# Triangular solves on GpSimd, spare buffers for two heads, and the S5 setup's copies on ScalarE, in a decoder trunk

## The chip, the core and the metric

The kernel runs on one core of a Trainium2 chip. The core has a matrix engine (TensorE, PE), a vector engine (VectorE, DVE), a scalar engine (ScalarE, ACT), GpSimd (POOL) and SyncE (SP), which issues most of the transfers. The metric is the time of one execution in microseconds on the device. Before the change three runs took 1185.95 to 1189.26 us, median 1188.44.

## The reference

One layer of a hybrid decoder trunk on 1024 tokens of width 1024, in float32. A normalised input is projected once into the inputs of three branches: an RG-LRU, a gated DeltaNet (GDN) with 8 heads of 128, and a diagonal complex state space (S5). Their outputs go through gates, are joined, projected back, added to the input, and a small gated embedding follows. What matters here is the GDN head:

```python
kb = kc * bc[..., None]
a_kk = jnp.where(strict, jnp.einsum('nbhid,nbhjd->nbhij', kb, kc) * decay, 0.0)
lhs = a_kk + jnp.eye(c, dtype=jnp.float32)
sol = lax.linalg.triangular_solve(lhs, rhs, left_side=True, lower=True, unit_diagonal=True)
u_c, w_c = sol[..., :dv], sol[..., dv:]
...
def step(state, inp):
    v_new = u_i - jnp.einsum('bhcd,bhde->bhce', w_i, state)
    o_i = (q_i * exp(gc_i)) @ state + aqk_i @ v_new
    state = state * jnp.exp(g_last)[..., None, None] + jnp.einsum('bhcd,bhce->bhde', k_dec, v_new)
    return state, o_i
_, o = lax.scan(step, state0, (qc, kc, u_c, w_c, a_qk, gcum))
```

The scan is a chain: a step needs the state of the step before. The triangular systems and the products with q and k don't depend on the state.

## The kernel before

The kernel holds its data with the channel in the partition. A projection block (`project`) is 48 matmuls of 128x512 in fp32r: 8 slices of the width, three products each (high half by high half, low by high, high by low), for two halves of the tokens; its operands are called hhi, hlo, whi, wlo and its result pp. The blocks of the RG-LRU and S5 inputs come first, with the S5 branch computed between them, then the blocks k 0, 1, 2, q 0, v 0 and z 0, and then, head by head in `gdn`, k of head h+3, q, v and z of head h+1.

Between the matmuls of a projection a planner, written into the kernel itself, puts all other work. It prices each instruction (`price`), keeps a modelled time for each engine (`account`), and at each projection matmul (`fill`, `tick`) advances the tasks whose modelled inputs are there, by priority (`PRIO`). `need(tasks)` lets the projections stop until the tasks named are done. A task yields a letter for the lane on which it goes on ("v" DVE, "a" ACT, "g" GpSimd, "pe" PE, "d" transfers). The order that comes out is fixed on every engine, so each engine takes its instructions strictly in that order. Every change in a price, an engine or a wait moves the order of everything behind it.

For a GDN head the tasks are these.
- `project_conv` evacuates a block into raw, after a fill of three columns on GpSimd (L486), and runs a convolution of four taps on DVE (L477); the SiLU on ACT gives kT or qT.
- `k_post` makes AT on DVE (L1131) and writes the 32x32 diagonal blocks of two heads to memory.
- `solve(h0)`, for two heads at a time, inverts the diagonal blocks in 31 rounds of a multiplication (L1156) and a subtraction (L1159) on 64 partitions. Round j works on n x m elements with n = j+1, m = 31-j; over all rounds that is 5,456 elements twice. It runs on DVE before (SOLVE_G = 8, that is for no head on GpSimd). GpSimd prepares W with a fill and a mask (L1147, L1148).
- `levels(h)` builds the inverse of the whole 128x128 blocks from them on PE (matmuls M,XT and Xs,AT; Xs is written by DVE, L1234).
- `chain(h)` is the recurrence, two chunks of 64 at a time, so eight steps t: Sm·kT on PE, R on DVE (L1293), XT·R on PE, V on DVE (L1305), V·kd on PE, and the new Sm on DVE (L1317). The parts of the output, Sm·qT and V·AQ, stand beside them on PE. I call each passage from DVE back to PE a hop: three per step.

`gdn` calls `need(*prev)`, with prev the chain of head h, ahead of k_proj(h+3) and q_proj(h+1): the four buffers of kT and two of qT are reused, and at h = 1 they belong to head 0. So k_proj(4) and q_proj(2) start when chain(0) is done.

The S5 setup (`s5_base`) computes small tables on DVE; its 17 copies and sign changes are `cpy` (L803) and `ng` (L802). The gates are in `gates`: two products with gg on PE, then egl, ekd, egc on ACT (L585 to L589); they use the single PSUM buffer pc, as the transposes of s_Q (L902 copies them out) do. Before the convolution of S5 the input u goes to memory and back in another layout (ud, s_U), and the kernel row Kp becomes the Toeplitz matrices s_MT. `decay` makes the masks of the GDN decay: it loads gcb and masks it on GpSimd (L609).

## Time and profile before

The profiled execution took 1193.25 us; its span is 1191.5 us, the rest lies around the span. The granted clock of TensorE is 0.968 in the mean.

| | before |
|---|---|
| median of 3 runs | 1188.44 us |
| profiled execution | 1193.25 us |
| its span | 1191.5 us |
| PE busy | 1112.1 us (93%) |
| DVE busy | 784.9 us (66%) |
| ACT busy | 565.7 us (47%) |
| GpSimd busy | 158.8 us (13%) |
| mean granted clock | 0.968 |

PE is busy nearly all the time. Its 79 us of idle time stand in a few places, 9.1 of them at the very start. The clock of PE is at its full level (2.4 GHz) for most of the span and at the half (1.2 GHz) in some stretches after idle time. When PE has little to do its clock falls, and the first matmuls of what follows run at the low clock; in the rows below such a tail is seen from the duration of a 128x512 matmul, 0.63 us instead of 0.40.

In a row of the timeline the first number is the start in us from the start of the span, the second is the duration, then engine, line, operation, output and inputs, shape, and how many like it follow each other. In brackets stands the idle time of the engine before it, and what ended it.

### The profile page before, as it was taken

To read this page: it belongs to the slowest core of one execution; us is meant where nothing else is said; L and a number is where in the kernel's file an instruction comes from. 1 tells how busy PE (TensorE), PEld (TensorE's weight loads), DVE (VectorE), ACT (ScalarE), POOL (GpSimd) and SP (SyncE) were. 2 spreads that over 40 slices of the span, in tenths; PEclk is the share of its full clock that TensorE was granted. 3 is DMA by queue.
4 is the path that set the end of the run, shared out by engine and by line. 5 is a ranking of instruction groups with operands and counts; after the bars stand their busy time and mean duration, and the time that the engine had idled before them with its cause. 6 is when DMAs were issued, how large, how long until landed. Compare 5 with 4: busy or idle time off the path is not lost. (4 is left out here: it accounts for less than half of the span.)

```text
span 1191.5 us, 17246 instructions
## 1 busy us (share of the span) xinstructions
PE 1112.1 (93%) x6165; PEld 903.9 (76%) x6165; DVE 784.9 (66%) x1933; ACT 565.7 (47%) x1138; POOL 158.8 (13%) x166
## 2 busy tenths in 40 slices
PE   6889688999989899999999999999989899999996
PEld 4677476777878677788888888878867688878885
DVE  6787576857578786786678667865655444263665
ACT  6533536634767784244543545344663143253332
POOL 1100000000011010000000010000053042044441
PEclk9999889999989999699999999999999999999999
DMA  8311354555567331122222221212355564464222
GB/s 301 119 36 45 99 134 140 144 152 132 157 192 210 115 125 33 48 71 54 94 67 72 54 94 32 89 33 74 117 161 211 194 212 159 142 210 134 71 90 88
DMA packets 85222, 140.18 MB, mean 118 GB/s; under 512 B 31760, under 2 KB 42192, under 8 KB 85136
## 3 DMA queue, kind: packets, MB, share of 16 engines
q1 hardware_dynamic: 83984, 134.88, 36.7%
q0 software_dynamic: 1152, 4.19, 0.9%
q8 instruction: 49, 0.80, 0.3%
q14 instruction: 37, 0.30, 0.1%
HBM read 97.98 MB, written 31.49 MB: 109 GB/s over the span
## 5 line engine op out<-in xcount | busy, mean ns | idle before, releaser
L195 PE MATMUL pp<-hhi,whi 128*128 128x512 f32 x768 | 316.3, 412 | 4.4 <-ACT hhi L404 2.3
L195 PE MATMUL pp<-hlo,whi 128*128 128x512 f32 x768 | 314.3, 409 | 3.1 <-DVE hlo L407 3.1
L195 PE MATMUL pp<-hhi,wlo 128*128 128x512 f32 x768 | 315.1, 410 | 1.8 <-DVE wlo L425 1.8
L195 PEld LDWEIGHTS pp<-hhi,whi 128*128 128x128 f32 x768 | 147.4, 192 | 35.9 <-ACT hhi L404 3.3
L195 PEld LDWEIGHTS pp<-hlo,whi 128*128 128x128 f32 x768 | 147.1, 192 | 33.4 <-DVE hlo L407 4.0
L195 PEld LDWEIGHTS pp<-hhi,wlo 128*128 128x128 f32 x768 | 147.1, 191 | 30.9 <-issue 2.4
L477 DVE SCALAR_TENSOR_TENSOR cy<-raw,c_gdn_conv_w,cy 128x512 f32<-128x512 f32 x144 | 108.2, 752 | 15.0 <-ACT cy L473 12.2
L1508 DVE TENSOR_TENSOR mhl<-mr,mhl 128x512 fp32r<-128x512 f32 x64 | 61.5, 963 | 76.4 <-ACT mhl L1506 76.3
L195 PE MATMUL pg<-ws,mhl 128*128 128x512 f32 x384 | 102.6, 401 | 0.2 <-DVE mhl L1508 0.2
L425 DVE TENSOR_TENSOR wlo<-wraw,whi 128x1024 fp32r<-128x1024 f32 (+1 forms) x52 | 62.5, 1201 | 47.0 <-ACT whi L423 45.4
L1508 POOL TENSOR_TENSOR ws<-wsr,ws 128x512 fp32r<-128x512 f32 x48 | 67.2, 1403 | 181.7 <-ACT ws L1506 181.5
L195 PEld LDWEIGHTS pg<-ws,mhl 128*128 128x128 f32 x384 | 72.3, 190 | 18.0 <-DVE mhl L1508 1.0
L195 PE MATMUL pp<-ws,fth 128*128 128x512 f32 x256 | 81.3, 397 | 0.0
L1506 ACT CAST mhl<-mr 128x512 fp32r<-128x512 f32 x64 | 39.8, 621 | 77.3 <-DMA mr<-mix 45.6
L487 ACT COPY raw<-pp 128x512 f32<-128x512 f32 x56 | 32.7, 584 | 82.6 <-PE pp L195 82.5
L423 ACT CAST whi<-wraw 128x1024 fp32r<-128x1024 f32 (+1 forms) x52 | 52.7, 1014 | 26.5 <-DMA wraw<-in_w_blk 26.0
L195 PE MATMUL pp<-ws,mhl 128*128 128x512 f32 x192 | 53.3, 405 | 5.3 <-ACT mhl L1506 2.6
L195 PEld LDWEIGHTS pp<-ws,fth 128*128 128x128 f32 x256 | 48.0, 188 | 10.9
L1506 ACT CAST ws<-wsr 128x512 fp32r<-128x512 f32 x48 | 29.8, 623 | 54.2 <-DMA wsr<-in_w_out 22.9
L1331 ACT ACTIVATE osq<-on 128x128 f32<-128x128 f32 x64 | 19.8, 309 | 70.5 <-DVE on L1328 53.7
L195 PE MATMUL pp<-ws,ftl 128*128 128x512 f32 x128 | 51.1, 400 | 0.0
L195 PEld LDWEIGHTS pp<-ws,mhl 128*128 128x128 f32 x192 | 35.5, 190 | 15.5 <-ACT mhl L1506 3.0
(414 smaller groups left out, 2018.1 us busy)
## 6 DMA issues: line engine op xcount, KB each, us to landing
wraw<-in_w_blk SPq DMA_DIRECT2D x48, 512.0 KB, 4.2
mr<-mix SPq DMA_DIRECT2D x64, 256.0 KB, 3.0
dec<-dec SPq DMA_DIRECT2D x16, 512.0 KB, 4.5
wsr<-in_w_out SPq DMA_DIRECT2D x32, 256.0 KB, 2.9
xt<-in_xT SPq DMA_DIRECT2D x16, 256.0 KB, 5.9
ppd<-po POOLq DMA_DIRECT2D x8, 512.0 KB, 3.4
gcb<-grow SPq DMA_DIRECT2D x8, 512.0 KB, 4.8
dec<-gcb SPq DMA_DIRECT2D x8, 512.0 KB, 2.8
```

The costliest lines, as they stand in the source:

```text
L195: self.nc.tensor.matmul(**kw)
L423: nc.scalar.copy(out=hi, in_=raw)
L425: nc.vector.tensor_tensor(out=lo, in0=raw, in1=hi.bitcast(F32), op=ALU.subtract)
L477: nc.vector.scalar_tensor_tensor(out=y[:, sl], in0=raw[:, j + sl.start:j + sl.stop], scalar=wconv[:, j:j + 1], in1=y[:, sl], op0=ALU.mult, ...
L487: nc.scalar.copy(out=raw[:, 3 + 512 * half:3 + 512 * half + 512], in_=ps)
L1331: nc.scalar.activation(out=sq, in_=on[:, t, :], func=AF.Square, accum_out=d["so"][:, t:t + 1])
L1506: nc.scalar.copy(out=hl[:, 0, :], in_=raw)
L1508: e.tensor_tensor(out=hl[:, 1, :], in0=raw, in1=hl[:, 0, :].bitcast(F32), op=ALU.subtract)
```

## The change

There are three parts.

1. `SOLVE_G` is 0 instead of 8: all four `solve` tasks emit their 62 operations to GpSimd instead of DVE.
2. `extra` gives three buffers of the size of kT from a pool of their own ("more"). Head 4 takes its kT and head 2 its qT from it, and the gates of the S5 output projection (`glu`) take the three that were in a pool "gsig". At h = 1 `need(*prev)` is asked for only ahead of v_proj(2), not ahead of k_proj(4) and q_proj(2). For the other heads the order of calls stays. `q_post(h)` now also waits for chain(h-2), the last reader of q's second-level buffer.
3. In `s5_base` the four fills of 1.0 and 0.0 go to GpSimd, and the 17 copies and sign changes to ScalarE, with `yield` of the lane so that the planner counts them there.

```diff
--- before.py
+++ after.py
@@ -29,7 +29,7 @@
 HEADS = 8
 GATE = 0
 SHARED = (3, 7)
-SOLVE_G = 8
+SOLVE_G = 0
 SQRT_2PI = 0.7978845608028654
 
 
@@ -272,6 +272,9 @@
     def slot(self, tag, shape, name, dtype=F32):
         return self.wk.tile(shape, dtype, name=name, tag=tag, bufs=SLOTS[tag])
 
+    def extra(self, shape, name):
+        return self.more.tile(shape, F32, name=name, tag="more", bufs=3)
+
     def consts(self, pool):
         nc = self.nc
         c = pool.tile([P, P], F32, name="ident")
@@ -785,9 +788,14 @@
         v.tensor_tensor(out=ki, in0=t1, in1=den, op=m)
         self.s5k = (kr, ki)
         yield
+        yield "g"
         pr, pi = wide[:, :, 0:9], wide[:, :, 9:18]
-        v.memset(pr[:, :, 0:1], 1.0)
-        v.memset(pi[:, :, 0:1], 0.0)
+        nc.gpsimd.memset(pr[:, :, 0:1], 1.0)
+        nc.gpsimd.memset(pi[:, :, 0:1], 0.0)
+        ca, sa = (keep.tile([P, 16, 8], F32, name=z) for z in ("s_ca", "s_sa"))
+        nc.gpsimd.memset(ca[:, :, 0:1], 1.0)
+        nc.gpsimd.memset(sa[:, :, 0:1], 0.0)
+        yield "v"
         v.tensor_tensor(out=pr[:, :, 1], in0=er, in1=cs, op=m)
         v.tensor_copy(out=pi[:, :, 1], in_=im)
         tp1, tp2 = wide[:, :, 18:22], wide[:, :, 22:26]
@@ -799,8 +807,9 @@
         K = lambda n, w: keep.tile(sh + [w], F32, name=n)
         Aq, Bq, Ag, Bg = K("s_Aq", 8), K("s_Bq", 8), K("s_Ag", 9), K("s_Bg", 9)
         H0, H1 = slice(0, 64), slice(64, 128)
-        ng = lambda o, i_: v.tensor_scalar(out=o, in0=i_, scalar1=-1.0, scalar2=None, op0=m)
-        cpy = lambda o, i_: v.tensor_copy(out=o, in_=i_)
+        ng = lambda o, i_: nc.scalar.mul(out=o, in_=i_, mul=-1.0)
+        cpy = lambda o, i_: nc.scalar.copy(out=o, in_=i_)
+        yield "a"
         cpy(Aq[H0], pr[H0, :, 0:8])
         cpy(Aq[H1], pi[H1, :, 0:8])
         ng(Bq[H0], pi[H0, :, 0:8])
@@ -816,6 +825,7 @@
         cpy(c8, cs)
         cpy(s8, sn)
         cpy(R8, er)
+        yield "v"
         for _ in range(3):
             v.tensor_tensor(out=t1, in0=s8, in1=s8, op=m)
             v.scalar_tensor_tensor(out=s8, in0=s8, scalar=2.0, in1=c8, op0=m, op1=m)
@@ -823,22 +833,22 @@
             v.tensor_tensor(out=c8, in0=c8, in1=t1, op=ALU.subtract)
             v.tensor_tensor(out=R8, in0=R8, in1=R8, op=m)
             yield
+        yield "a"
         cb, sb = (keep.tile([P, 16, 16], F32, name=z) for z in ("s_cb", "s_sb"))
-        ca, sa = (keep.tile([P, 16, 8], F32, name=z) for z in ("s_ca", "s_sa"))
         for o, z in ((cb, c8), (sb, s8)):
             for hs, g4 in ((H0, slice(0, 4)), (H1, slice(4, 8))):
                 cpy(o[hs, :, 0].rearrange("p (i g) -> p i g", i=4), z[hs].rearrange("p (i g) -> p i g", i=4)[:, :, g4])
-        yield
+        yield "v"
         flat = wide.rearrange("p a b -> p (a b)")
         u, w = (flat[:, 128 * z:128 * z + 128].rearrange("p (g k) -> p g k", g=16) for z in range(2))
         for n in (1, 2, 4, 8):
             bc = lambda a: a[:, :, n - 1:n].to_broadcast([P, 16, n])
             self.cmul(v, cb[:, :, n:2 * n], sb[:, :, n:2 * n], cb[:, :, :n], sb[:, :, :n], bc(cb), bc(sb), u[:, :, :n], w[:, :, :n])
             yield
-        v.memset(ca[:, :, 0:1], 1.0)
-        v.memset(sa[:, :, 0:1], 0.0)
+        yield "a"
         cpy(ca[:, :, 1], cb[:, :, 15])
         cpy(sa[:, :, 1], sb[:, :, 15])
+        yield "v"
         for n, e in ((1, 1), (2, 2), (4, 3)):
             bc = lambda a: a[:, :, n:n + 1].to_broadcast([P, 16, e])
             self.cmul(v, ca[:, :, n + 1:n + 1 + e], sa[:, :, n + 1:n + 1 + e], ca[:, :, 1:1 + e], sa[:, :, 1:1 + e],
@@ -1069,7 +1079,7 @@
 
     def k_proj(self, h):
         nc, d = self.nc, self.hd[h]
-        kT = d["kT"] = self.slot("kT", [P, S], "kT")
+        kT = d["kT"] = self.extra([P, S], "kT") if h == 4 else self.slot("kT", [P, S], "kT")
 
         def act(y, raw, sl):
             nc.scalar.activation(out=kT[:, sl], in_=y[:, sl], func=AF.Silu)
@@ -1163,13 +1173,13 @@
 
     def q_proj(self, h):
         nc, d = self.nc, self.hd[h]
-        qT = d["qT"] = self.slot("qT", [P, S], "qT")
+        qT = d["qT"] = self.extra([P, S], "qT") if h == 2 else self.slot("qT", [P, S], "qT")
 
         def act(y, raw, sl):
             nc.scalar.activation(out=qT[:, sl], in_=y[:, sl], func=AF.Silu)
             yield
         y, raw, cv = self.project_conv(8 + h, self.gcw[:, h, :], None, act)
-        d["q"] = self.spawn(self.q_post(h, cv), "d", after=cv[:1] + [d["k"]])
+        d["q"] = self.spawn(self.q_post(h, cv), "d", after=cv[:1] + [d["k"]] + ([self.hd[h - 2]["chain"]] if h > 1 else []))
 
     def q_post(self, h, cv):
         nc, d = self.nc, self.hd[h]
@@ -1363,15 +1373,18 @@
                                     lambda: self.room(self.psc) and self.room(self.pso) and self.room(self.psa))
             d["fin"] = self.spawn(self.finish(h), "v", [d["chain"], d["z"]])
             if h + 3 < HEADS:
-                self.need(*prev)
+                if h != 1:
+                    self.need(*prev)
                 self.k_proj(h + 3)
                 if h % 2 == 0:
                     hd[h + 2]["solve"] = hd[h + 3]["solve"] = self.spawn(self.solve(h + 2), "d", [hd[h + 2]["k"], hd[h + 3]["k"]])
             if h + 1 < HEADS:
                 n = hd[h + 1]
                 n["levels"] = self.spawn(self.levels(h + 1), "g", [n["solve"], d["levels"]] + prev)
+                if h != 1:
+                    self.need(*prev)
+                self.q_proj(h + 1)
                 self.need(*prev)
-                self.q_proj(h + 1)
                 self.v_proj(h + 1)
                 self.need(*([hd[h - 1]["fin"]] if h else self.decays))
                 if h == HEADS - 2:
@@ -1401,7 +1414,7 @@
             self.decs -= 1
             zs.append((hi, lo))
 
-    def glu(self, zs, bg, gs):
+    def glu(self, zs, bg):
         nc = self.nc
 
         def pre(i, box):
@@ -1422,7 +1435,7 @@
             wh, wl = self.take(("g", i))
             if i == 3:
                 self.need(last)
-            sig = self.slot("kd", [P, P, 8], "gs") if i == 3 else gs.tile([P, P, 8], F32, name="gs", bufs=3)
+            sig = self.slot("kd", [P, P, 8], "gs") if i == 3 else self.extra([P, P, 8], "gs")
             box = []
             pr = self.spawn(pre(i, box), "d", t[-1:] + [last])
             for half in range(2):
@@ -1744,7 +1757,7 @@
                 self.k_proj(1)
                 self.k_proj(2)
                 self.need(*tiles, *outs)
-            with tc.tile_pool(name="gdn", bufs=1) as self.gp:
+            with tc.tile_pool(name="gdn", bufs=1) as self.gp, tc.tile_pool(name="more", bufs=1) as self.more:
                 hd = self.hd
                 bg = self.load(cp, "s5_b_glu", [P, 4])
                 hd[0]["solve"] = hd[1]["solve"] = self.spawn(self.solve(0), "d", [hd[0]["k"], hd[1]["k"]])
@@ -1760,10 +1773,9 @@
                 self.spawn(self.wstream(), "d", [prep])
                 self.spawn(self.mstream(), "d", [prep])
                 self.need(prep)
-                with tc.tile_pool(name="gsig", bufs=1) as gs:
-                    self.glu(zs, bg, gs)
-                    self.out_proj()
-                    self.ple(cp)
+                self.glu(zs, bg)
+                self.out_proj()
+                self.ple(cp)
 
 
 def layout(x, norm_g, w_in, rg_lambda, gdn_a_log, gdn_dt_bias, **kw):
```

In the planned order of PE, this is the middle of chain(0), two of its steps, before. R, V and Sm are the results of DVE that the matmul waits for.

```order
L195 MATMUL pc<-R,XT 128x128
L195 MATMUL pc<-V,kd 128x128
L195 MATMUL po<-V,AQ 128x128
L195 MATMUL pc<-Sm,kT 128x128
L195 MATMUL po<-Sm,qT 128x128
L198 MATMUL pg<-ident,kT 128x128
L195 MATMUL pc<-R,XT 128x128
L195 MATMUL pc<-V,kd 128x128
```

And the same place after the change, from a product with R on.

```order
L195 MATMUL pc<-R,XT 128x128
L195 MATMUL pp<-hhi,wlo 128x512
L195 MATMUL pp<-hhi,whi 128x512
L195 MATMUL pp<-hlo,whi 128x512
L195 MATMUL pp<-hhi,wlo 128x512
L195 MATMUL pp<-hhi,whi 128x512
L195 MATMUL pp<-hlo,whi 128x512
L195 MATMUL pc<-V,kd 128x128
L195 MATMUL po<-V,AQ 128x128
L195 MATMUL pp<-hhi,wlo 128x512
L195 MATMUL pp<-hhi,whi 128x512
L195 MATMUL pp<-hlo,whi 128x512
```

Projection matmuls stand between the hops: before, eight in all between the hops of chain(0), after, 75. The last five hops of chain(0) still hold none after the change; this is its end.

```order
L195 MATMUL pp<-hhi,wlo 128x512
L195 MATMUL pc<-Sm,kT 128x128
L195 MATMUL po<-Sm,qT 128x128
L198 MATMUL pg<-ident,kT 128x128
L195 MATMUL pc<-R,XT 128x128
L195 MATMUL pc<-V,kd 128x128
L195 MATMUL po<-V,AQ 128x128
L195 MATMUL pc<-Sm,kT 128x128
L195 MATMUL po<-Sm,qT 128x128
L195 MATMUL pc<-R,XT 128x128
L195 MATMUL po<-V,AQ 128x128
L195 MATMUL pp<-hhi,whi 128x512
```

In GpSimd's order this is the beginning of solve(0) before: the mask of W (L1148), then fills of raw and masks of decays, since the solve's own operations stand on DVE.

```order
L1148 AFFINE_SELECT sW<-sW 64x1024
L486 MEMSET raw 128x3
L609 AFFINE_SELECT gcb<-gcb 128x1024 x2
L486 MEMSET raw 128x3 x2
L609 AFFINE_SELECT gcb<-gcb 128x1024
L486 MEMSET raw 128x3
```

After the change (lines are those of the changed file: L1166 and L1169 are the solve's multiplication and subtraction, L612 the mask of a decay, L489 the fill of raw) the operations of the solve stand in the same queue.

```order
L1166 TENSOR_TENSOR sT<-sW,sA 64x135
L1169 TENSOR_TENSOR sW<-sW,sT 64x5x27
L1166 TENSOR_TENSOR sT<-sW,sA 64x156
L1169 TENSOR_TENSOR sW<-sW,sT 64x6x26
L612 AFFINE_SELECT gcb<-gcb 128x1024
L1166 TENSOR_TENSOR sT<-sW,sA 64x175
L1169 TENSOR_TENSOR sW<-sW,sT 64x7x25
L1166 TENSOR_TENSOR sT<-sW,sA 64x192
L1169 TENSOR_TENSOR sW<-sW,sT 64x8x24
```

The masks of the decays come after the 6th, the 14th and within the 19th round of the solve, and fills of raw stand in between. In PE's order around the gates' product, before (ident,gc and ident,s_Q are transposes into pc and po):

```order
L195 MATMUL pp<-hhi,wlo 128x512
L195 MATMUL pc<-gg,upper 128x64
L195 MATMUL pc<-gg,ones 128x64
L195 MATMUL pp<-hhi,whi 128x512
L195 MATMUL pp<-hlo,whi 128x512
L195 MATMUL pp<-hhi,wlo 128x512
L195 MATMUL pp<-hhi,whi 128x512
L195 MATMUL pp<-hlo,whi 128x512
L195 MATMUL pp<-hhi,wlo 128x512
L198 MATMUL pc<-ident,s_Q 128x128 x4
L198 MATMUL pc<-ident,gc 64x128
L198 MATMUL po<-ident,s_Q 128x128 x4
```

After the change this is the same place.

```order
L195 MATMUL pp<-hhi,wlo 128x512
L195 MATMUL pp<-hhi,whi 128x512
L195 MATMUL pp<-hlo,whi 128x512
L195 MATMUL pp<-hhi,wlo 128x512
L198 MATMUL pc<-ident,s_Q 128x128 x4
L195 MATMUL pp<-hhi,whi 128x512
L195 MATMUL pp<-hlo,whi 128x512
L198 MATMUL pc<-ident,gc 64x128
L195 MATMUL pp<-hhi,wlo 128x512
L198 MATMUL po<-ident,s_Q 128x128 x4
```

The two products with gg are gone from there: they stand 33 projection matmuls ahead of the transposes of s_Q, six before the change. Two projection matmuls stand between the first transposes of s_Q and that of gc.

## Rows read from the trace of the kernel before

**Rows 1.** The page: busy time, share of the span and instructions of each engine.
```profile
PE 1112.1 (93%) x6165; PEld 903.9 (76%) x6165; DVE 784.9 (66%) x1933; ACT 565.7 (47%) x1138; POOL 158.8 (13%) x166
```
**Rows 2.** Stretches: us, busy time (count) by engine, PEclk, DMA share, GB/s.
```profile
475.00:500.00 25.00, 21.76 (x80) 16.85 (x79) 17.66 (x64) 6.86 (x25) 0.00 (x0) 0.59 0.21 58
```
**Rows 3.** Waits of PE: us in total, times, longest.
```profile
PE pc L195 <- DVE V L1305: 4.4, 9, 0.9
PE pg L198 <- DVE AT L1131: 4.4, 4, 3.3
...
PE pc L198 <- ACT egl L585: 2.2, 1, 2.2
```
**Rows 4.** Timeline of PE, chain(0) and the end of it.
```profile
471.73 0.49 PE L195 MATMUL pc<-Sm,kT 128*128 128x128 f32 x2
...
473.55 0.49 PE L195 MATMUL pc<-R,XT 128*128 128x128 f32 x2
...
476.71 0.79 PE L195 MATMUL pc<-R,XT 128*128 128x128 f32 x2
...
483.01 0.79 PE L195 MATMUL pc<-Sm,kT 128*128 128x128 f32 x2
...
486.79 0.79 PE L195 MATMUL pc<-Sm,kT 128*128 128x128 f32 x2
...
493.60 0.77 PE L195 MATMUL pp<-hhi,whi 128*128 128x512 f32 x1
...
495.66 0.63 PE L195 MATMUL pp<-hlo,whi 128*128 128x512 f32 x1
```
**Rows 5.** Timeline of PE, one step of chain(1).
```profile
566.06 0.38 PE L195 MATMUL pc<-Sm,kT 128*128 128x128 f32 x2
...
570.53 0.40 PE L195 MATMUL pp<-hhi,whi 128*128 128x512 f32 x1
570.76 0.38 PE L195 MATMUL pc<-Sm,kT 128*128 128x128 f32 x2
```
**Rows 6.** Timeline of PE in the S5 stage.
```profile
138.87 0.35 PE L195 MATMUL po<-s_G,s_Q 128*16 128x112 f32 x2
...
150.26 0.77 PE L195 MATMUL pg<-s_U,s_QT 128*128 128x128 f32 x2 [9.91 <-DMA s_MT<-s_Kp]
```
**Rows 7.** Timeline of PE, end of chain(5).
```profile
802.43 0.46 PE L195 MATMUL po<-V,AQ 128*128 128x128 f32 x2 [0.54 <-DVE V L1305]
```
**Rows 8.** Timeline of DVE in the S5 setup.
```profile
72.65 0.30 DVE L803 COPY s_Ag<-s_w 64x288 f32<-64x288 f32 x1
...
81.40 1.23 DVE L425 TENSOR_TENSOR wlo<-wraw,whi 128x1024 fp32r<-128x1024 f32 x1 [4.66 <-ACT whi L423]
```
**Rows 9.** Groups by line, DVE and GpSimd: busy, mean ns, idle before.
```profile
L1156 DVE TENSOR_TENSOR sT<-sW,sA 64x31 f32<-64x31 f32 (+15 forms) x124 | 41.7, 336 | 2.2 <-DMA sA<-adiag 0.7
...
L1413 POOL TENSOR_TENSOR gg<-gg,gz 128x1024 f32<-128x1024 f32 x4 | 9.6, 2402 | 22.3 <-DMA gg<-sgd 12.1 <-DVE ort L312 10.2
```
**Rows 10.** Timeline of GpSimd, a multiplication of 512 elements.
```profile
1099.30 1.30 POOL L1621 TENSOR_TENSOR fgt<-fgt,fpp 128x512 f32<-128x512 f32 x1 [2.52 <-ACT fgt L1662]
```
**Rows 11.** Timeline of DVE and PE, end of solve(0) and levels(0).
```profile
442.77 0.21 DVE L1159 TENSOR_TENSOR sW<-sW,sT 64x31 f32<-64x31 f32 x1
...
452.60 0.69 PE L195 MATMUL pg<-Xs,AT 32*32 32x32 f32 x30 [0.69 <-DVE Xs L1234]
```
**Rows 12.** Timeline of GpSimd, the third decay mask.
```profile
426.80 1.17 POOL L609 TENSOR_SCALAR_AFFINE_SELECT gcb<-gcb 128x1024 f32<-128x1024 f32 x1 [9.94 <-DVE cy L477]
```
**Rows 13.** Timeline of GpSimd and DVE, two overlaps.
```profile
384.45 1.62 POOL L1148 TENSOR_SCALAR_AFFINE_SELECT sW<-sW 64x1024 f32<-64x1024 f32 x1
384.87 1.22 DVE L312 TENSOR_TENSOR krt<-krt,kss 128x8 f32<-128x8 f32 x1
...
875.10 1.30 POOL L1508 TENSOR_TENSOR ws<-wsr,ws 128x512 fp32r<-128x512 f32 x1 [1.42 <-ACT ws L1506]
875.81 0.34 DVE L1293 SCALAR_TENSOR_TENSOR R<-pc,negc,vn 128x128 f32<-128x128 f32 x1
```

## The prediction

> **What bounds the kernel now.** I read the engines' busy times first: the matrix engine (PE) works 1112.1 of 1191.5 us, so 79 us of idle PE are all that a change of order can win, beside stretches in which its clock is low [rows 1]. Second, busy time and clock by 25 us stretches, to find where that idle time is. From 500 to 850 us PE is nearly full. The worst stretch is 475 to 500: PE counts as 21.76 us busy, but at a granted clock of 0.59, so it does much less than it seems [rows 2]. Third, PE's list of waits. Those on V of the chain, on AT and on egl are the ones that this change touches [rows 3]. Last, the matmuls of that worst stretch one by one: the recurrence of head 0 (chain(0)) runs there with nothing beside it. Its six last steps take from 471.73 to 493.60, 21.9 us, without one projection matmul. At full clock a step takes 3.16 us (473.55 to 476.71), once the clock has gone to half 3.78 us (483.01 to 486.79), because each product waits for VectorE (DVE) and DVE for it; and a projection matmul behind it, at 495.66, still takes 0.63 us [rows 4]. A step with projections between its products costs PE far less: in the chain of head 1 one takes 4.70 us (566.06 to 570.76) and holds 15 projection matmuls of 0.23 us (570.53 to 570.76), so the step itself adds 4.70 - 15 x 0.23 = 1.25 us; such a projection matmul shows 0.40 us, so one at half clock costs about 0.2 more [rows 4, 5]. Projections are work that has to be done anyway: what is moved between the steps costs nothing there.
>
> **The change part by part.**
>
> D, chain(0). k_proj(4) and q_proj(2) no longer wait for chain(0), since kT of head 4 and qT of head 2 get spare buffers. By the order, the hops of chain(0) hold 75 projection matmuls where they held 8. Six filled steps cost 6 x 1.25 = 7.5 us. The fill runs out before the end: five hops in a row at the end of chain(0) hold none, 1.7 steps, which take 5.3 us at full clock and 6.4 at half clock [rows 4] with 2.1 us of their own work among it; so 3.2 to 4.3 us of stall stay, I take 3.7. Gain 21.9 - 7.5 - 3.7 = 10.7 us. The tail at half clock behind it stays.
>
> E, head 1. The blocks that fill chain(0) are gone from where they stood. Four hops at the end of chain(1) hold no projection now: 4/3 of a step, 4.2 us at full clock with 1.5 of work [rows 4], 2.7 us lost, and a tail of about six matmuls at half clock, each 0.2 us longer, 1.2. Loss 3.9 us.
>
> F, heads 3 and 5. Their bare ends (one stands in the rows, a wait of 0.54 on V [rows 7]) are filled by the new order. All waits on V make 4.4 us in nine [rows 3], six of them, of 0.54 each, in chain(0); 1.2 us are left for these, and one clock tail, 1.2. Gain 2.4 us.
>
> A, gates of the S5 stage. The two products with gg stood six projections ahead of the transposes of s_Q, which need the same bank; they stand 33 ahead now (7.6 us). The wait on egl, 2.2 us [rows 3], and a tail of six matmuls at half clock, 1.2, go: 3.4 us. What is late next is the copy s_QT, for which nothing changes. B, the copy of u to its layout: eight projections instead of four lie between Kp's product (138.87) and the one that waits 9.9 us for s_MT (150.26) [rows 6]; the chain of transfers between them is the same, so 4 x 0.23 = 0.9 us. C, the first attention matrices: the transposes of qT stand eight projections (1.8 us) later and their wait on AT is 3.3 us [rows 3]; the solve's small operations no longer stand in DVE's queue there, which may take the rest of the wait, and a clock tail of eight matmuls, 1.6. Between 1.8 and 4.8; I take 2.3, near the lower end, because the matrices themselves still come from DVE.
>
> S5 setup. 17 copies and sign changes of 0.16 to 0.31 us and four fills leave DVE, 4.1 us. DVE goes on to sit idle 4.66 us for whi just behind them [rows 8], so this is worth nothing by itself, nor does it cost: the longest way is a change of engine each time, and that idle time covers it. If it were not there, some eight changes of engine at a few tenths would cost 2 us. It only moves the planner's order (A, B).
>
> X, the solves. This is the part with a price. All four triangular solves move from DVE to GpSimd. On DVE the multiplications are 124 in 41.7 us [rows 9], the subtractions the same: 20.8 us per solve. GpSimd needs 1.30 us for 512 elements per partition [rows 10] and 2.40 for 1024 [rows 9]: 2.15 ns an element and 0.2 fixed. A solve has 62 operations and 10,912 elements: 62 x 0.2 + 23.5 = 36 us alone. That is the lower bound, since rows of 1 to 31 elements, a gap between dependent operations, and the shared access of both engines come on top; if every operation waits 0.3 us, half a convolution operation, 55 us. I take 45. The Trainium skill (GPSIMD Engine Reference, section 3.1) gives 1.96 times VectorE's time for such an operation, which would make it an estimated 41 us; it is a rule against this move, and by it the sum below would not change. On DVE the last operation of solve(0) ended at 442.98, and PE came to its levels 9.6 us later, with a wait of 0.69 at 452.60 [rows 11]; so a solve has some room. In GpSimd's queue the last third of solve(0) now stands behind the third masking of a decay (gcb, L609), which came at 426.80 [rows 12]; then 12 pairs of operations follow, 14 us alone, 20 with the additions: end 441 to 447 against 443. PE reaches the levels about as early as before. I expect 0 to 3 us of wait there, the same for solve(2), which no longer shares DVE with chain(0) but has least room, and less for the other two, which have 3 to 8 us. A term more: fills of three columns (L486) for the convolutions stand between the solve's operations, and DVE waits for them in order. Together -4 us, between 0 and -10.
>
> Sum: 3.4 + 0.9 + 2.3 + 10.7 - 3.9 + 2.4 = 15.8, less 4 is 11.8 us. The profiled execution took 1193.25 us, its span 1191.5; with the change 1181.4. The median of the runs is 4.8 lower, 1188.44, so I predict 1188.4 - 11.8 = 1176.6, rounded 1176 us. With X at 0 and C at 4.8 it is 1170, with X at -10 and A gone as well 1186.
>
> **The rivals.**
>
> GpSimd is too slow (slower than before). One mechanism: the end of a solve. levels(h) on PE waits for it, and so does the store of xdiag on the transfer queue of SyncE, behind which the next weights stand. Room is about 10 us over 45, so it decides from a solve of some 55 us on. If short rows cost as much again as the elements (23.5 more), a solve takes about 70 to 75 us and each of the four puts 10 to 15 us on PE: plus 40 to 60, less the 15.8 gained, 1213 to 1233; with half of that excess about 1200. For it: no row shows GpSimd on rows this short. Against it: fills and masks on 64 partitions with rows of 32 do not take twice as long there (1.62 us with the other engine in the way [rows 13]).
>
> Contention takes the gain (about no change). While GpSimd masked sW (384.45, 1.62 us), a DVE operation of 8 elements that reads two tiles of SBUF took 1.22 us at 384.87, and ended with it. R, which reads one operand from PSUM, took its usual 0.34 us at 875.81 in the middle of a GpSimd multiplication [rows 13]. So the convolutions (three operations of 0.75 us for each half), the low halves of the weights and small products of norms wait; R, V and Sm wait only behind them, DVE being in order. Around 250 operations of up to 0.75 us each now run on GpSimd. If each of the 24 hops of a chain that runs beside a solve takes 0.3 us more, that is 7 us per head; where projections fill the hops it is hidden, so I count one to two heads, 8 to 12 us: 1184 to 1189. The Trainium skill (SBUF — State Buffer, section "Who interferes with whom") states this as a lock held for the whole instruction when both read SBUF, and none for a VectorE operation with one SBUF input; the two pairs of rows agree, and that rule alone cannot say how many of the waits reach PE.
>
> Better than forecast: the solves' departure frees DVE (83 us of its 785) and other waits behind it go as well, C in full and half of what stays in D and E: 6 to 12 more, 1164 to 1170.
>
> That it does not do what it says: the order shows the projections between the hops of chain(0), so the fill itself is certain; only its worth is open.
>
> **How the numbers follow.** The forecast, 1170 to 1184, 0.58; contention, 1184 to 1192, 0.17; too slow a GpSimd, 1195 to 1235, 0.13; better, 1160 to 1170, 0.12. The range 1164 to 1192 leaves out the slow case and a third of the best one. A measurement of this kernel tells some 0.3% from no change, 3.6 us: faster is below 1184.9. Faster 0.58 + 0.12 + 0.04 = 0.74, the same 0.11, slower 0.15.
>
> **What would show it.** D is right if chain(0) shows projections between its products at a clock near 1.0 and the stretch that held 475 to 500 is full. E shows as four bare hops at the end of chain(1), F as none at the ends of heads 3 and 5. A shows as no wait on egl. X shows in GpSimd's rows: mean time of L1156 and L1159 about 0.65 us, a solve 40 to 50 us, and few waits of PE on Xs. Contention would show as DVE's convolution operations at 1 us and more and as waits on V and Sm in filled steps. The prediction is wrong if a solve takes over 55 us, or if PE's waits on Xs, V and Sm grow by more than 10 us.

## The result: 1178 us, faster by about one per cent

The changed kernel took 1178.03 us (median of four runs, 1170.78 to 1178.40) against 1188.85 us before (1185.95 to 1191.91): a ratio of 0.9891, interval 0.9851 to 0.9930, which is 8 to 18 us less. The forecast was 1176 us, range 1164 to 1192. The profiled execution of the changed kernel took 1178.4 us with a span of 1176.7 us.

The first line of the changed kernel's page answers to [rows 1]: VectorE is busy 55 us less, GpSimd 158 us more, and PE's idle time inside the span falls from 79 to 74 us.

```profile
PE 1102.6 (94%) x6165; PEld 896.4 (76%) x6165; DVE 730.2 (62%) x1664; ACT 569.1 (48%) x1155; POOL 316.3 (27%) x418
```

The stretches around chain(0) answer to [rows 2]; the columns are the same. chain(0) runs from 459 to 498 now. The stretch that counted 21.76 us busy at a clock of 0.59 is now one at 0.87, and the next one has fallen to 0.92: the low place is shorter, but it hasn't gone.

```profile
450.00:475.00 25.00, 25.00 (x295) 20.86 (x295) 14.25 (x59) 12.58 (x32) 2.49 (x4) 1.00 0.03 5
475.00:500.00 25.00, 20.70 (x109) 16.94 (x109) 19.81 (x60) 10.24 (x27) 15.51 (x29) 0.87 0.33 97
500.00:525.00 25.00, 23.56 (x130) 19.82 (x129) 20.57 (x47) 9.73 (x36) 22.45 (x35) 0.92 0.16 48
```

PE's waits, for [rows 3]. The wait on egl is gone, that on V has fallen from 4.4 us to 1.4; that on AT has hardly moved (3.3 before, 2.9 for the longest), that on s_MT from 9.9 [rows 6] to 8.6, and a wait on Sm is new.

```profile
PE pg L195 <- DMA s_MT<-s_Kp: 8.6, 1, 8.6
...
PE pg L198 <- DVE AT L1141: 3.2, 2, 2.9
...
PE pc L195 <- DVE Sm L1327: 2.2, 3, 1.7
...
PE pc L195 <- DVE V L1315: 1.4, 3, 0.9
...
PE pg L195 <- DVE Xs L1244: 0.6, 1, 0.6
```

The transposes of s_Q, which waited 2.21 us for egl, follow the projections without a wait, and that of gc waits 0.20 us where it waited 0.68. Timeline of PE:

```profile
116.06 0.60 PE L198 MATMUL pc<-ident,s_Q 128*128 128x128 f32 x4
...
117.33 0.30 PE L198 MATMUL pc<-ident,gc 128*64 128x128 f32 x1 [0.20 <-ACT s_QT L912]
```

The steps of chain(0) on PE's timeline, for [rows 4]. From 473.35 to 478.26 a filled step takes 4.91 us with projections between its products, at full clock; it holds 16 of them, so the step itself adds 4.91 - 16 x 0.23 = 1.23 us, as in chain(1) before. From 489.59 on there are none: five hops take 9.0 us until the next projection at 498.59, and the last of them are at half clock (0.80 for a pair that takes 0.49). Eleven projection matmuls behind them are still at half clock (the tenth is the last line here); before the change it was six.

```profile
473.35 0.38 PE L195 MATMUL pc<-Sm,kT 128*128 128x128 f32 x2
...
478.26 0.38 PE L195 MATMUL pc<-Sm,kT 128*128 128x128 f32 x2
...
489.59 0.38 PE L195 MATMUL pc<-Sm,kT 128*128 128x128 f32 x2
...
491.44 0.46 PE L195 MATMUL pc<-V,kd 128*128 128x128 f32 x2 [0.53 <-DVE krt L315]
...
493.78 0.80 PE L195 MATMUL pc<-Sm,kT 128*128 128x128 f32 x2 [1.65 <-DVE Sm L1327]
495.41 0.80 PE L195 MATMUL po<-Sm,qT 128*128 128x128 f32 x2 [0.83 <-DVE on L1338]
496.84 0.80 PE L195 MATMUL pc<-R,XT 128*128 128x128 f32 x2 [0.64 <-DVE R L1303]
498.17 0.77 PE L195 MATMUL po<-V,AQ 128*128 128x128 f32 x2 [0.53 <-ACT whi L426]
498.59 0.77 PE L195 MATMUL pp<-hhi,whi 128*128 128x512 f32 x1
...
503.22 0.63 PE L195 MATMUL pp<-hhi,whi 128*128 128x512 f32 x1
```

### The profile page after: what moved, and what is told of

Read it like the earlier page. It is cut to its first block, busy times and chain, and to the rows that moved or that the text cites. A ratio compares the mean times of both kernels' runs of the same rounds, so it can differ in the third digit from the quotient of the medians.

```text
span 1176.7 us, 17257 instructions
## 1 busy us (share of the span) xinstructions
PE 1102.6 (94%) x6165; PEld 896.4 (76%) x6165; DVE 730.2 (62%) x1664; ACT 569.1 (48%) x1155; POOL 316.3 (27%) x418
## 5 line engine op out<-in xcount | busy, mean ns | idle before, releaser
L480 DVE SCALAR_TENSOR_TENSOR cy<-raw,c_gdn_conv_w,cy 128x512 f32<-128x512 f32 x144 | 116.2, 810 | 29.5 <-ACT cy L476 15.5
L1166 POOL TENSOR_TENSOR sT<-sW,sA 64x31 f32<-64x31 f32 (+15 forms) x124 | 77.4, 624 | 80.4 <-DMA sA<-adiag 71.1
L428 DVE TENSOR_TENSOR wlo<-wraw,whi 128x1024 fp32r<-128x1024 f32 (+1 forms) x52 | 64.9, 1248 | 45.0 <-ACT whi L426 43.9
L1169 POOL TENSOR_TENSOR sW<-sW,sT 64x31 f32<-64x31 f32 (+15 forms) x124 | 81.3, 656 | 9.4
L195 PE MATMUL pp<-ws,fth 128*128 128x512 f32 x256 | 81.3, 396 | 0.0
L1315 DVE TENSOR_SCALAR V<-pc,bp 128x128 f32<-128x128 f32 x64 | 22.3, 349 | 56.5 <-PE pc L195 56.1
L195 PEld LDWEIGHTS pp<-ws,fth 128*128 128x128 f32 x256 | 48.0, 188 | 10.9
```

The costliest lines, as they stand in the source:

```text
L195: self.nc.tensor.matmul(**kw)
L428: nc.vector.tensor_tensor(out=lo, in0=raw, in1=hi.bitcast(F32), op=ALU.subtract)
L480: nc.vector.scalar_tensor_tensor(out=y[:, sl], in0=raw[:, j + sl.start:j + sl.stop], scalar=wconv[:, j:j + 1], in1=y[:, sl], op0=ALU.mult, ...
L1166: e.tensor_tensor(out=tv, in0=W[:, :n, j:j + 1].to_broadcast([64, n, m]), in1=A[:, j:j + 1, j + 1:].to_broadcast([64, n, m]), op=ALU.mult)
L1169: e.tensor_tensor(out=W[:, :n, j + 1:], in0=W[:, :n, j + 1:], in1=tv, op=ALU.subtract)
L1315: v.tensor_scalar(out=V, in0=p2, scalar1=bp[:, t:t + 1], scalar2=None, op0=ALU.mult)
```

## The experiments

All ratios are to the kernel before, measured beside it on the same chip; its median was 1184.7 to 1188.9 us there. I call a hop bare when no projection matmul stands in it. Two quantities are taken from the profiles. One is the time from the last write of s_X, the end of the S5 stage, to the first mhl of the output projection, on VectorE; I call it the time of the heads. The other is PE's lost time in a stretch: the stretch less, for each matmul in it, the distance that its kind has to the next one when nothing is in the way (the lower third of those distances over five of the traces). About 4 us per head remain in every kernel, so differences count, not the values; and another way to tell the kinds apart moves a single value by up to 1.5 us. A stretch "head h" goes from the first V of chain(h) to that of the next chain.

### The three parts, each alone, and two of them

S5 part alone: the hunks of `s5_base`, nothing else.

> Only the copies, sign changes and fills of the S5 setup move; solves stay on VectorE, no spare buffers. In the planned order nothing changes from the convolutions of the GDN heads on, but the gates' products and the transposes around 120 us do. In the profile of the full change the heads start 9.3 us earlier than before, of which about 5 us are waits of PE that the order removes (egl 2.2, s_QT 0.7, s_MT 1.3, a clock tail of 0.8); the rest is not explained. Theory: the S5 part alone gives 4 to 9 us, 1180 to 1185. Rival: the earlier start is a difference between two executions and the S5 part gives nothing, 1188.

Measured: 0.9963, 0.9945 to 0.9981. The S5 part gives 4.4 us (2 to 6.5), as its theory has it. The wait on egl, 2.21 us, stands in all three profiles without the S5 part and in none of the eleven with it. The run also shows that the 9.3 us by which the heads start earlier in the profile of the full change are not all due to the order: from the first projection to the last s_X it took 300.1 us in the profile of the kernel before, but 294.5 and 296.2 in two kernels below whose S5 setup is unchanged, against 290.8 to 292.2 in the first four profiles with the change. About half of the 9 us belongs to that one profiled execution. Over all eleven profiles with the change, which have one order of PE in this stage, it is 288.8 to 295.1 us; so the gain of the S5 part is shown by the ratio of many runs, not by single profiles.

Spare buffers alone:

```diff
+        kT = ... self.extra([P, S], "kT") if h == 4 else self.slot("kT", [P, S], "kT")
+        qT = ... self.extra([P, S], "qT") if h == 2 else self.slot("qT", [P, S], "qT")
+                if h != 1:
+                    self.need(*prev)
```

> Only the spare buffers for kT of head 4 and qT of head 2 and the two waits dropped at h = 1; solves on VectorE, S5 setup as before. By the order chain(0) has 1 bare hop instead of 18, but chain(1) gets 11 bare hops where it had none. Theory: the blocks that fill chain(0) are missing from chain(1), so that most of the gain is given back: 17 hops less at 0.84 us each (a bare step of 3.78 us against 1.25 filled, a third of it per hop) minus 11 more, about 5 us gained, less a clock tail of 1.2: 1184 to 1186. Rival: the stall of chain(0) is worth 10.7 us by itself, as the prediction had it before its loss in chain(1): 1178.

Measured: 1.0027, 1.0010 to 1.0044: slower. Neither number was right, but the mechanism was the theory's, with a larger price: PE's lost time in head 0 fell by 10.9 us and that of head 1 rose by 14.7 (table below). Its timeline of PE shows where: a product of chain(1) waits 3.32 us for V, because the low half of a weight (1.23 us) and operations of solve(2) stand ahead of V on VectorE, and from 538.91 to 555.92 the end of chain(1) is bare.

```profile
506.87 0.46 PE L195 MATMUL pc<-V,kd 128*128 128x128 f32 x2 [3.32 <-DVE V L1308]
...
538.91 0.49 PE L195 MATMUL pc<-R,XT 128*128 128x128 f32 x2 [0.26 <-DVE R L1296]
539.93 0.46 PE L195 MATMUL pc<-V,kd 128*128 128x128 f32 x2 [0.53 <-DVE V L1308]
...
548.11 0.77 PE L195 MATMUL pc<-V,kd 128*128 128x128 f32 x2 [0.53 <-ACT XT L1258]
...
551.13 0.79 PE L195 MATMUL pc<-Sm,kT 128*128 128x128 f32 x2
...
554.17 0.79 PE L195 MATMUL pc<-R,XT 128*128 128x128 f32 x2
555.50 0.76 PE L195 MATMUL po<-V,AQ 128*128 128x128 f32 x2 [0.54 <-DVE V L1308]
555.92 0.77 PE L195 MATMUL pp<-hhi,whi 128*128 128x512 f32 x1
```

Solves alone:

```diff
-SOLVE_G = 8
+SOLVE_G = 0
```

> Only the four solves move to GpSimd; buffers, waits and the S5 setup as before. By the order chain(0) has 22 bare hops instead of 18 and the ends of chain(3) and chain(5) have none instead of 5. Theory: 4 hops more cost 3 us, the filled ends give 4, contention for SBUF costs 3 to 5: 1188 to 1193, no gain. Rival 1: freeing 83 us of VectorE is what pays, 1180. Rival 2: a solve of 45 to 60 us is late for its levels, PE waits on Xs, 1195 or more.

Measured: 0.9991, 0.9965 to 1.0016, no difference. Both rivals fall: freeing VectorE of 83 us is worth nothing by itself, and no solve is late (PE's waits on Xs make 0.6 us, 2.1 before).

S5 part and spare buffers, solves on VectorE:

```diff
-SOLVE_G = 0
+SOLVE_G = 8
```

> The full change with the solves on VectorE again: S5 part and spare buffers stay. By the order chain(0) has 1 bare hop, chain(1) 11, chain(3) and chain(5) 3 each. Theory: gains of the S5 part and of the spare buffers add up, 1176 to 1181, so the move of the solves is worth about 0 to 4 us with the spare buffers (it spreads 11 bare hops of chain(1) to 5 and 5, fills heads 3 and 5, and pays with contention). Rival: the solves on GpSimd carry the gain, without them 1186 or more.

Measured: 0.9998, 0.9979 to 1.0016. The theory (1176 to 1181) was wrong by as much as it was for the spare buffers alone: 0.9963 x 1.0027 = 0.9990, so these two do add up. The rival's number came true: without the solves on GpSimd nothing is gained.

> The full change once more, beside the next three on the same chip. S5 part alone gave 0.9963, spare buffers alone 1.0027, solves alone 0.9991, S5 part and spare buffers 0.9998. Theory: the parts don't add up (their sum would be 0.998): the spare buffers only pay when the solves are off VectorE, because with the solves on it the bare steps move from chain(0) to chain(1). Then the full change repeats its 0.985 to 0.993, some 8 us under the sum of its parts. Rival: its first measurement was lucky and it comes out at the sum, 0.996 to 0.999.

Measured: 0.9884, 0.9845 to 0.9923 (1173.39 us against 1184.74). The gain is there again. The three parts alone make 0.9963 x 1.0027 x 0.9991 = 0.998, about 2 us; together they give 11 to 14. The difference is an interaction of spare buffers and solves, and the lost time of PE shows its place (us; "heads" is the time of the heads):

| kernel | head 0 | head 1 | head 3 | head 5 | heads |
|---|---|---|---|---|---|
| before | 18.4 | 4.5 | 4.4 | 8.2 | 514.4 |
| S5 part alone | 18.9 | 5.4 | 4.1 | 9.7 | 515.6 |
| spare buffers alone | 7.5 | 19.2 | 4.1 | 8.1 | 519.6 |
| S5 part and spare buffers | 7.2 | 18.1 | 4.3 | 8.3 | 515.5 |
| solves alone | 21.5 | 4.0 | 3.8 | 4.5 | 512.2 |
| full change | 13.4 | 12.5 | 4.6 | 4.3 | 508.4 |
| full change, again | 13.8 | 12.8 | 4.4 | 5.9 | 507.4 |

With the solves on VectorE the spare buffers only move the bare steps from chain(0) to chain(1): heads 0 and 1 lose 22.9 us before and 26.7 with them, 3.8 more. The solves alone cost 2.6 there (25.5) and give 3.7 in head 5. Both together lose 25.9 in heads 0 and 1, where the two effects would add up to 29.3: with the solves on GpSimd the planner places the blocks so that each of the two chains has 5 bare hops, instead of 1 and 11. That would be a place for 3.4 us of the interaction; reckoned from the two rows that hold the S5 part (24.3 and 25.3) it is 2.0. It is not shown that the 5 and 5 bare hops make the gain: the full change loses no less in heads 0 and 1 than S5 part and spare buffers do (25.9 and 25.3), and the next run has 1 and 11 and almost the time of the heads of the full change (508.9). The time of the heads shows more of the interaction (519.6 or 515.5 with spare buffers, 512.2 with the solves, 508 with both); where it lies stays open.

### Which solves

```diff
-SOLVE_G = 0
+SOLVE_G = 4
```

> The full change, but only solves 4 and 6 on GpSimd; solves 0 and 2 are back on VectorE. By the order chain(0) has 1 bare hop, chain(1) 11, as with all solves on VectorE, and the ends of chain(3) and chain(5) have none, as in the full change. Theory: what the two late solves give is the filled ends of heads 3 and 5, 4 us; what makes the spare buffers pay is the move of solves 0 and 2. So 0.9998 (S5 part, spare buffers, no solves) less 0.0035: 0.995 to 0.998, about 8 us slower than the full change. Rival: the late solves carry most of the gain, 0.990.

Measured: 0.9957, 0.9938 to 0.9976, as the theory has it. By the ratios the two late solves give 0.9998 to 0.9957, about 5 us, and the move of solves 0 and 2 with the spare buffers 0.9957 to 0.9884, 8 to 9 us. The profiles place little of the second step. The time of the heads is 508.9 us here and 503.8 to 508.4 in the four profiles that have PE's order of the full change, and heads 0 and 1 together lose no more than in the two profiles of the full change itself. Longer as well are the S5 stage, 295.1 us against 289.4 to 293.2 in those four with the same order of PE, and one wait for mhl in the output projection, 5.4 us against 2.2 to 2.6. So what solves 0 and 2 give on GpSimd is seen in the ratio, and its cause is not shown.

### What the contention costs

In each solve, rounds 2 to 30 were replaced by fills, which read nothing; the inversion is left out there. The fills came out shorter than what they replace, 28.1 us in a solve where the operations take 38 to 41, and solves 2, 4 and 6 take 32 to 41 us instead of 43 to 46, so the whole times differ by more than the reads. At the bare end of chain(0) fills run beside all five hops.

```diff
+            if 0 < j < 30:
+                for _ in range(2):
+                    e.memset(fk[:, :108 + round(1.94 * n * m)], 0.0)
+                    yield
+                continue
```

> The full change, but in each solve rounds 2 to 30 are replaced by fills of about the same length on GpSimd, which read nothing; what is left out is the inversion of the diagonal blocks. The planned order of every other instruction on PE is the same. Theory: VectorE's operations with two operands in SBUF wait for GpSimd's reads; with fills they don't, the convolutions take 0.75 us again in the mean instead of 0.81, the bare end of chain(0) takes 5.5 to 6.5 us instead of 8.6, and the time falls by 3 to 5 us, to about 0.988 of the kernel before if the full change gives 0.991. Rival: contention is hidden behind the projections, no change in the time.

First the full change at the bare end of chain(0): VectorE, then GpSimd, the same microseconds.

```profile
491.84 1.17 DVE L480 SCALAR_TENSOR_TENSOR cy<-raw,c_gdn_conv_w,cy 128x512 f32<-128x512 f32 x1 [0.47 <-ACT cy L476]
492.93 0.53 DVE L317 SCALAR_TENSOR_TENSOR kry<-krt,kry 128x8 f32<-128x8 f32 x1
493.39 0.34 DVE L1327 SCALAR_TENSOR_TENSOR Sm<-Sm,egl,pc 128x128 f32<-128x128 f32 x1
493.64 1.03 DVE L480 SCALAR_TENSOR_TENSOR cy<-raw,c_gdn_conv_w,cy 128x512 f32<-128x512 f32 x1
494.60 0.56 DVE L313 SCALAR_TENSOR_TENSOR krt<-kry 128x8 f32<-128x8 f32 x1
...
492.54 0.90 POOL L1166 TENSOR_TENSOR sT<-sW,sA 64x220 f32<-64x220 f32 x1
...
494.20 0.93 POOL L1166 TENSOR_TENSOR sT<-sW,sA 64x231 f32<-64x231 f32 x1
```

A convolution operation takes 1.17 and 1.03 us there, and operations of 8 elements 0.53 and 0.56, while GpSimd's solve operations beside them take 0.90 and 0.93 where their neighbours take 0.61. Each of the two operations of 8 elements ends within 0.03 us of the GpSimd operation beside it (493.46 and 493.44, 495.16 and 495.13). Sm, queued behind them, comes late, and the product that needs it waits 1.65 us. With fills on GpSimd the same operations take 0.75 and 0.16 (VectorE):

```profile
489.96 0.75 DVE L485 SCALAR_TENSOR_TENSOR cy<-raw,c_gdn_conv_w,cy 128x512 f32<-128x512 f32 x1 [0.47 <-ACT cy L481]
490.63 0.16 DVE L322 SCALAR_TENSOR_TENSOR kry<-krt,kry 128x8 f32<-128x8 f32 x1
490.71 0.34 DVE L1338 SCALAR_TENSOR_TENSOR Sm<-Sm,egl,pc 128x128 f32<-128x128 f32 x1
490.96 0.74 DVE L485 SCALAR_TENSOR_TENSOR cy<-raw,c_gdn_conv_w,cy 128x512 f32<-128x512 f32 x1
```

and the same five hops on PE take 6.65 us (487.72 to 494.37) where the full change needs 8.58 (489.59 to 498.17):

```profile
487.72 0.38 PE L200 MATMUL pc<-Sm,kT 128*128 128x128 f32 x2
...
489.57 0.46 PE L200 MATMUL pc<-V,kd 128*128 128x128 f32 x2 [0.54 <-DVE krt L320]
...
491.10 0.49 PE L200 MATMUL pc<-Sm,kT 128*128 128x128 f32 x2 [0.85 <-DVE Sm L1338]
492.04 0.73 PE L200 MATMUL po<-Sm,qT 128*128 128x128 f32 x2 [0.45 <-DVE on L1349]
493.04 0.80 PE L200 MATMUL pc<-R,XT 128*128 128x128 f32 x2 [0.27 <-DVE R L1314]
494.37 0.77 PE L200 MATMUL po<-V,AQ 128*128 128x128 f32 x2 [0.53 <-DVE bp L1138]
```

The convolutions fall from 810 ns in the mean to 763:

```profile
L485 DVE SCALAR_TENSOR_TENSOR cy<-raw,c_gdn_conv_w,cy 128x512 f32<-128x512 f32 x144 | 109.4, 763 | 29.2 <-ACT cy L481 25.9 <-issue 2.0 <-POOL sT L1177 0.7
```

All operations that VectorE has in both the kernel before and the changed one take 20 us longer in sum in the full change, and 2 us longer with the fills. Lost time in head 0 falls from 13.4 to 9.8 us. Yet the whole takes 0.9879 (0.9851 to 0.9907) against 0.9884, medians 1170.38 and 1173.39 us: the 3 to 5 us of the theory aren't shown by the time, and the time of the heads (507.1) is that of the full change. The contention is real, 2 to 4 us at the bare end, and what it costs in all is within what these runs can tell, 0 to 4 us.

### How long a solve may take

A fill between the two operations of each round makes the solves longer, with the order of everything else as in the full change.

```diff
+            e.memset(fk[:, :108 + round(1.94 * n * m)], 0.0)
```

> The full change, but in each round of the four solves a fill that reads nothing stands between the multiplication and the subtraction, about as long as one of them; the planner prices it at nothing, so that the order of everything else is the same. A solve of 43 to 45 us becomes one of some 62 us (solve(0), with its waits for decay masks, 59 becomes up to 77). In the profile of the full change PE comes to the levels 12, 15, 22 and 17 us after the end of solves 0, 2, 4 and 6; in the kernel before the way from the end of solve(0) to the levels took 8.7 us with a wait of PE at its end. So the room is about 3, 6, 13 and 8 us, 30 in all. Theory: 4 x 18 = 72 us more, less 30: some 35 to 45 us are lost, 1.02 to 1.03 of the kernel before, with PE waits on Xs. Rival: fills of raw behind the longer solve stop VectorE's convolutions too, over 1.04. Second rival: the solves have much more room than that, under 1.00.

Measured: 0.9871, 0.9837 to 0.9905, no loss. The expectation was wrong in its first step: the solves became 51 to 54 us long (solve(0) 63), not 62, since a fill also covers the gap between two dependent operations. With up to three times the fill:

> As the longer solves, but the fill in each round is up to three times as long (27 us of fills per solve instead of 13.6), the order of everything else the same. The first version made a solve 51 to 54 us long, not 62, since a fill also covers the gap between two dependent operations, and cost nothing: PE came to the levels 7.1 to 13.6 us after the end of a solve, without a wait. Now a solve should take about 65 us (solve(0) up to 76). Theory: the room is used up; of the 13.5 us more, at most 0, 0, 6 and 3 us fit, so that PE waits some 13, 13, 7 and 10 us for the levels: 35 to 45 us lost, 1.02 of the kernel before, with waits on Xs or on the fill of XT. Rival: there is still room and it stays under 0.995.

Measured: 1.027, 1.0197 to 1.0343, 1218.9 us. The solves take 61, 65 and 65 us and solve(0) 71, and PE waits for what follows them; waits on Xs were 0.6 us in the full change. Waits of PE:

```profile
PE pg L198 <- DVE Xs L1249: 15.8, 6, 7.0
...
PE pc L198 <- DVE V L1320: 6.5, 5, 3.1
```

So the point from which the length of a solve decides lies between 54 and 61 us.

### Filling the end of chain(1) too

```diff
-        kT = ... self.extra([P, S], "kT") if h == 4 else ...
+        kT = ... self.extra([P, S], "kT") if h in (4, 5) else ...
-                if h != 1:
+                if h not in (1, 2):
                     self.need(*prev)
                 self.k_proj(h + 3)
```

> The full change, and the third spare buffer also takes kT of head 5, so that k_proj(5) doesn't wait for chain(1). By the order chain(1) has 1 bare hop instead of 5; chain(0) keeps its 5. Theory: the bare end of chain(1), about 2.7 us of stall and 1.8 of clock tail in the profile of the full change, goes: 4 us less than the full change, if no new bare place shows up (chain(7) gets one hop). Rival: the block is missing elsewhere, no gain.

Measured: 0.9906, 0.9877 to 0.9936, beside 0.9884 for the full change on the same chip: no gain that shows. Head 1 lost 6.1 us instead of 12.5, as expected, and the time of the heads is 505.0; but from there to the end it took 331.8 us in this profile, against 330.9 and 327.6 in the two of the full change. Whether the order does that or the execution is open.

> As the one before, but solve(0) on VectorE, the other three on GpSimd. By the order chain(0) has 1 bare hop instead of 5 and chain(1) 1. Theory: the bare end of chain(0), 8.6 us in the full change for 2.1 us of work, goes too: 8 to 10 us less than the full change, about 0.983 of the kernel before. Rival: solve(0) on VectorE delays the convolutions and the levels of head 0 (waits on Xs of 1.5 us are back) and half of it is lost.

Measured: 0.9853, 0.9827 to 0.9880, 1167.79 us against 1173.39 for the full change on the same chip. It is the fastest version here, though its interval overlaps that of the full change. Head 0 lost 4.3 us instead of 13.4, the time of the heads is 502.1. Head 1 lost 13.3, of it two waits of 2.9 and 3.0 us on a crowded VectorE:

```profile
PE pg L198 <- DVE AT L1141: 6.1, 3, 3.0
...
PE pg L198 <- DVE on L1356: 3.3, 2, 2.9
```

> The full change, the third spare buffer for kT of head 5, and only solves 4 and 6 on GpSimd, 0 and 2 on VectorE. By the order chain(0) has 1 bare hop, chain(1) to chain(5) none, chain(6) and chain(7) two each. With solve(0) alone on VectorE the profile showed two waits of PE of 2.9 and 3.0 us in chain(1), at 506 and 510, while solve(2) ran on GpSimd and VectorE's small operations took 0.5 us instead of 0.15. Theory: what matters are the bare hops, and the move of solves 0 and 2 pays only as long as no buffer fills chain(1); with the buffer, solves 0 and 2 are as good or better on VectorE: those two waits go, 0.981 to 0.985 of the kernel before. Rival: VectorE needs to be rid of solve(2), 0.988 or more.

Measured: 0.9943, 0.9917 to 0.9969. The theory is wrong, and the rival's number came true. Its reason is not shown: with solve(2) back on VectorE its operations stand ahead of V again (a wait of 3.28 us), but heads 0 and 1 together lose about 2 us less than in the run before. Longer are the S5 stage (294.3 us against 290.5, the same order on PE), the end of the heads, and the wait for mhl in the output projection (5.40 us against 2.58). Counting bare hops in the order alone doesn't give the time.

## Why the prediction was right, and where it was not

The total was right to 2 us (the sum gave 1176.6, which rounds to 1177); several terms were not, and that they made up for each other is luck. Measured one by one they give 4.4 (A and B) + 5.0 (D) - 8 (E) + 3.9 (F), 5.3 us, and with the forecast's 2.3 for C 7.6, of a gain of 11 to 14; the rest has no place in the profiles.

- **A and B** (4.3 us): 4.4 measured with the S5 part alone, right in sum. What the copies themselves cost was not measured apart.
- **C** (2.3): lost time between the last s_X and the first V is 16.6 us before, 13.0 and 11.6 with the full change. The size can't be told from the scatter: with the S5 part alone, whose order there is that of the kernel before, it is 14.3. The mechanism is at most half right: the wait on AT stayed at 2.9 us; waits on qT and Xs went.
- **D** (10.7): with the solves on VectorE the spare buffers gave 10.9 us in head 0. In the full change it is 5.0. The filled step was priced rightly (1.23 us for 1.25). The step that failed is the stall that stays at the end of chain(0): I took five bare hops as 5.3 to 6.4 us; they took 8.6, and 6.65 with fills on GpSimd, because the contention, which I had priced apart, falls on exactly these hops. The tail at half clock, which was to stay as it was, grew from six projection matmuls to eleven.
- **E** (-3.9): -8 us in head 1. The loss was twice what I had forecast: a fifth hop is bare in the middle of chain(1), part of chain(0)'s tail at half clock now falls into head 1, and about 1.4 us of waits on `on` and Sm are new at 519 to 522.
- **F** (2.4): 3.9 in head 5 (2.3 in the second profile of the full change), nothing in head 3.
- **X** (-4): the length of the solves was right: the mean operation takes 0.62 and 0.66 us (0.65 forecast), a solve 43.0, 44.9 and 45.7 us (45 forecast). Groups by line of the full change:

```profile
L1169 POOL TENSOR_TENSOR sW<-sW,sT 64x31 f32<-64x31 f32 (+15 forms) x124 | 81.3, 656 | 9.4
L1166 POOL TENSOR_TENSOR sT<-sW,sA 64x31 f32<-64x31 f32 (+15 forms) x124 | 77.4, 624 | 80.4 <-DMA sA<-adiag 71.1
...
L480 DVE SCALAR_TENSOR_TENSOR cy<-raw,c_gdn_conv_w,cy 128x512 f32<-128x512 f32 x144 | 116.2, 810 | 29.5 <-ACT cy L476 15.5 <-POOL raw L489 10.8 <-issue 2.0
```

solve(0) takes 59.1 us with its waits for the decay masks and ends at 435.7; the levels follow 12 us later without a wait. The 4 us put down for waits did not come: PE's waits on Xs are 0.6 us, 2.1 before. The prediction compared busy times and missed the more useful number: on VectorE, busy with a solve for some 20 us, a solve took 54 to 58 us from its first operation to its last, since other work of that queue stood between, so on GpSimd solves 2, 4 and 6 take less time than before. The first and last operation of solve(2), before and after, from the timelines of the two engines:

```profile
482.37 0.18 DVE L1156 TENSOR_TENSOR sT<-sW,sA 64x31 f32<-64x31 f32 x1 [0.71 <-DMA sA<-adiag]
...
536.12 0.20 DVE L1159 TENSOR_TENSOR sW<-sW,sT 64x31 f32<-64x31 f32 x1
```

```profile
482.41 0.23 POOL L1166 TENSOR_TENSOR sT<-sW,sA 64x31 f32<-64x31 f32 x1 [26.27 <-DMA sA<-adiag]
...
525.16 0.27 POOL L1169 TENSOR_TENSOR sW<-sW,sT 64x31 f32<-64x31 f32 x1
```

81.3 + 77.4 = 158.7 us of busy time against 83.3 on VectorE is 1.9 times. The Trainium skill's 1.96 for additions of 2048 elements (GPSIMD Engine Reference, section 3.1) is near it. The fills of raw behind the solve did stop VectorE once, for 10.8 us; PE's only wait near it is 0.89 us for raw at 428.22, and waits for raw make 1.1 us in all, 2.0 before. Timeline of VectorE:

```profile
426.84 1.08 DVE L480 SCALAR_TENSOR_TENSOR cy<-raw,c_gdn_conv_w,cy 128x512 f32<-128x512 f32 x1 [10.81 <-POOL raw L489]
```

- **The slow rival** had its point at some 55 us; it lies between 54 and 61, and with solves of 61 to 71 us the time is 1219 us, where 70 to 75 us were priced at 1213 to 1233. The place was right, the price somewhat low.
- **The contention rival**: seen, with a 2 to 4 us price at one place, not the 8 to 12 us that would have taken the gain. The rule of the Trainium skill (SBUF — State Buffer, section "Who interferes with whom") agrees with what was measured: two operands from SBUF against a reading GpSimd operation wait (0.53 us instead of 0.16), against a fill they don't. There the Trainium skill says "for the whole instruction" of VectorE's two-port modes; that the wait lasts until the GpSimd operation ends with two operands from SBUF too is seen from the two ends above (493.46 and 495.16).
- What the prediction did not see: that its parts aren't independent. It added D, E, F and X as if each could be had alone. Two of the three parts give nothing or lose by themselves, and that they pay together was in no term; by that the total is right for reasons that the prediction only partly had.

## What to carry to other kernels

A block that fills one stall is missing where it stood: count the bare hops of the whole order, before and after, and not only at the place that the change is about. Where a planner sets the order, undo each part by itself before crediting it; here two parts that are worth nothing alone give 8 us together. When parts have been undone, look also for the gain at the place that the argument names: here the ratios show a gain that the place doesn't. An engine half as fast as another may take serial work over if its end still lies ahead of the consumer; compare the time from first to last operation on both, since work that shares a queue takes longer than it is busy. The room can be measured by making the work longer until the time rises.

## What the runs showed that was not expected

Fills between dependent operations on GpSimd cost less than their own length: 14.5 us of fills per solve made it 8 us longer (solve(0) 4). About 0.08 us lie between the end of an operation and the start of the next one that depends on it (376.61 + 0.54 to 377.23 in the first round of solve(0)); a fill stands in half of these 61 gaps, which is 2.4 us of it, and the record has the fills begin and end inside the operations beside them. And executions of one order differ by up to 6 us in the S5 stage (294.5 to 300.1 us, and 288.8 to 295.1 with the changed setup), which is more than most terms of the sum: single profiles of this kernel can't be compared to less than that.
